# Values of dilation groups 1 and 2: strided token-major products, or feature-major products that are reordered and transposed

## The chip, the cores and the metric

The kernel runs on one core of one Trainium2 chip. The metric is device time in microseconds (us), from the start of the program to its end, as a median of several runs. Engines are named as the profile names them: PE is the matrix engine (PEld its loads of stationary operands, which run beside its products), DVE the vector engine, ACT the scalar engine, POOL GpSimd, and SP the engine that issues most transfers.

## The reference, cut to what matters

The program computes four layers on 512 tokens of 1024 features: a recurrent layer with dilated attention, a layer of sparse attention, and two layers with differential attention and 16 experts. The change touches the first layer alone. There each token gets 12 heads of 128 features in three groups of four; group 0 attends to neighbours, group 1 to every 4th token, group 2 to every 16th:

```
DIL_GROUPS = ((128, 1), (512, 4), (2048, 16))
h = rms_norm(x, norm_g) @ w_in
xa, za, q, k, v, zb, qm, zm = split_cols(h, HAWK_IN_SPLITS)
...
def to_sub(t):          # group gi, dilation dil
    t = t[:, :, gi * DIL_HEADS:(gi + 1) * DIL_HEADS]
    return t.reshape(b, sub, dil, DIL_HEADS, hd).transpose(0, 2, 3, 1, 4).reshape(
        b * dil, DIL_HEADS, sub, hd)
o, lse = banded_attention(to_sub(q)[:, :, None], to_sub(k), to_sub(v), ...)
```

So the values `v` of groups 1 and 2 are wanted with the tokens reordered: all tokens t with the same t mod 4 together.

## The kernel before

All float32 products with weights are made from two float32r parts: an operand is hi + lo, and a product is three matmuls, hi hi, hi lo and lo hi. `x` is kept feature-major, as 8 tiles of 128 features by 512 tokens, in both parts. Weights come by `wcols` in two chunks of 4 row tiles by 256 columns: SP loads a chunk into `wr` (4 buffers), ACT casts it to `wh` (L163, 3 buffers), DVE subtracts for `wl` (L164, 3 buffers).

There are two ways to multiply. `fm` (L184 to L186) takes the weights as the stationary operand and gives 128 columns of the weights on the partitions and 512 tokens along them: 24 matmuls of 512 moving columns fill one PSUM tile `pj`, two tiles a call. `tm2` (L211 to L213) takes 128 tokens of `x` as the stationary operand and 256 weight columns as the moving one: 48 matmuls of 256 columns fill one `pj` with two token tiles, token-major.

`dilated` runs twice (head slots 0 and 1, then 2 and 3; called spans here). A span makes queries and keys of group after group with `fm`, for which ACT (L667, L669) and DVE (L676, L678) copy PSUM to `dq` and `dk`; in groups 1 and 2 that copy also reorders the tokens to (t mod 4, t div 4), reading PSUM with a step of 4 elements. Scores and softmax follow. The weights of the three groups are then mixed through DRAM (`sd`, `wa`, L714 to L733). Then come the values, group 0, 1, 2 (L737 to L745): four token tiles a group, token-major, by `tm2`, which ACT copies to `dv` (L744). For groups 1 and 2 the stationary operand is a view of `x` that takes every fourth token: 128 elements with a step of 4 float32. Last come the transposes of the softmax tiles `de` (L759, copied by ACT to `pT`, L761), the products with the values into `po` (L769), and the gate `zw` by `fm`.

A scheduler sets the order on each engine from the order of the code and the dependences; pools hold 3 `pj` and 2 `pt` tiles of PSUM, and 26 tiles `t2` of 128 by 512 in SBUF.

Of the kernel before, what the change touches and what calls it, by code (L numbers as in the profile page):

```python
# [18 lines left out]
P = 128  # L19
# [29 lines left out]
class K:  # L49
# [11 lines left out]
    @contextmanager  # L61
    def phase(self, name, t2, e=(), r=0, pj=3, ps=2, pt=2, po=1):
        """Pools for one part of the network, with its numbers of tiles and of PSUM banks."""
# [16 lines left out]
    def xt(self):  # L80
        """A (hi, lo) pair of feature tiles."""
        t = self.wp.tile([P, 2, 512], F32R, name="x", tag="xt", bufs=8)
        return t[:, 0], t[:, 1]

    def x2(self):
        """A token tile [128, 1024] as two halves."""
        return [self.t2(F32, "x") for _ in range(2)]
# [29 lines left out]
    @contextmanager  # L117
    def after(self, marks):
        """Puts work on the engines of these instructions behind them."""
        with self.tc.issue_after(marks[0].ins), self.tc.issue_after(marks[1].ins):  # L120
            yield
# [16 lines left out]
    def behind(self):  # L138
        """The queue for a load, which goes behind the work of the last expert for a while."""
# [10 lines left out]
    def chunk(self, pieces, kt=4):  # L150
        """pieces: DRAM APs [kt*128, n], columns side by side (256 in all)."""
# [18 lines left out]
    def wcols(self, W, c0, n=256, k0=0, kt=8):  # L170
        """All row tiles of W[:, c0:c0+n] as [(hi, lo)] per row tile."""
# [9 lines left out]
    def mm3(self, ps, a, b, first, last):  # L181
        """ps += (a_hi + a_lo)^T (b_hi + b_lo), all but lo*lo."""
# [5 lines left out]
    def fm(self, w, x, n=512, cols=2):  # L188
        """Feature-major products: yields PSUM tiles [128 columns of W, n]."""
# [7 lines left out]
    def tm(self, w, x, ps):  # L197
        """Token-major product into ps [128 tokens, columns of w], for the feature tiles x of the tokens."""
# [4 lines left out]
    def tm2(self, w, x, toks, ps):  # L203
        """Token-major products of several token tiles side by side in ps, row tile by row tile."""
# [11 lines left out]
    def rsqrt(self, y, v, n):  # L216
        """y = v ** -0.5 on [128, n]."""
# [14 lines left out]
    def rms(self, xs, q=None, eps=1e-6):  # L232
        """rsqrt(mean(x^2) + eps) of token tiles xs (halves): [128, tiles], and as diagonal matrices; q is scratch."""
# [16 lines left out]
    def turn(self, out, x, diag=None):  # L250
        """out = x^T, or x^T diag."""
# [5 lines left out]
    def features(self, xs, i0, out, g=None, b=None, diag=None):  # L257
        """Two token tiles (halves), the first of them i0, to columns of the feature-major (hi, lo) tiles out, scaled by g
        (and b added); diag scales the tokens."""
# [33 lines left out]
    def constants(self):  # L293
        """The identity and the first norms' gains, then (after a yield) the other vectors."""
# [40 lines left out]
    def distances(self, causal):  # L335
        """Distance (or, if causal, 0) of key from query, and a far-off value where the key may not be seen."""
# [14 lines left out]
    def mem_x(self, name, gain, halves=None, pair=None):  # L351
        """The memory, normalised if gain is given (with the same factors at a second time), as feature-major (hi, lo)
        tiles [128, 256]."""
# [30 lines left out]
    def mem_kv(self, x, W, hd):  # L384
        """Keys of the 4 heads, [128, 256] (hi, lo) (64-wide heads doubled onto both halves), and values per memory tile."""
# [30 lines left out]
    def dup(self, ps, hs, ls):  # L416
        """Two 64-row heads in ps: each head's (hi, lo) doubled onto both partition halves."""
# [7 lines left out]
    def qstack(self, ps, scale, n=512):  # L425
        """Two 64-row heads in ps: per head a tile with its hi part on one half and its lo part on the other."""
# [11 lines left out]
    def scores(self, ps, q, kh, kl, i, n):  # L438
        """ps[:, :n] = scores of query tile i; q is a stack, or (hi, lo)."""
# [10 lines left out]
    def softmax_neg(self, e, ps, bias, m, l, scale=1.0):  # L450
        """e = exp(-scale (ps + bias) - max), l = its row sums; m keeps -max. ps holds negated scores / scale."""
# [5 lines left out]
    def mem_weights(self, q, kv, h):  # L457
        """Transposed weights of head h's attention over the memory."""
# [1497 lines left out]
```

## Time and profile before

| | |
|---|---|
| median of 3 runs | 3067.94 us |
| lowest and highest run | 3065.9 and 3076.09 us |
| span of the profiled execution | 3065.5 us |
| PE busy in it | 2933.4 us, 96% |
| DVE, ACT, POOL busy | 1944.0, 1555.6, 271.6 us |

The profiled execution has its times from the first to the last instruction; the median of the runs lies 2.4 us above that span. The two stretches in which the values of groups 1 and 2 are multiplied are 112.10 to 156.90 us and 283.32 to 328.12 us. PE starts a matmul before the one ahead of it has ended, so the time that one takes in a row of its kind is the distance of two starts, not the duration beside it.

### The profile page before, as it was taken

What the parts mean: (1) busy time and instruction counts of PE and PEld (TensorE: products, weight loads), DVE (VectorE), ACT (ScalarE), POOL (GpSimd) and SP (SyncE); (2) the same over time, 40 slices, a digit from 0 to 9 for tenths busy, and PEclk for the clock granted to TensorE, in tenths of its full rate; (3) what the DMA queues carried; (4) which work ended last, traced back from release to release, by engine and by line L of the source; (5) the groups of instructions that cost most, each with busy time, mean ns of one, the idle gap of its engine ahead of it and who ended that gap; (6) DMA issues with size and microseconds to landing.
All of it is one profiled execution on the core that took longest, in us unless ns stands there. A gap on an engine that the chain in (4) does not pass through costs nothing. (4 is left out here: it accounts for less than half of the span.)

```text
span 3065.5 us, 44383 instructions
## 1 busy us (share of the span) xinstructions
PE 2933.4 (96%) x16795; PEld 2500.5 (82%) x16795; DVE 1944.0 (63%) x3801; ACT 1555.6 (51%) x2717; POOL 271.6 (9%) x282
## 2 busy tenths in 40 slices
PE   8999999999999999999998999969999999699996
PEld 6989887986768999878798888759987878688874
DVE  4353357757756787443467877988744345777788
ACT  4243348546655455322345777735442233467774
POOL 0000000000000000000015200350000000270022
PEclk9999999999999999999999999989999999899998
DMA  4242132541105422222264999942222334369986
GB/s 135 67 143 77 52 114 93 180 135 35 46 21 180 127 63 63 83 93 93 90 204 140 323 327 338 318 142 63 63 76 90 96 110 158 120 242 323 331 323 239
DMA packets 335601, 453.49 MB, mean 148 GB/s; under 512 B 24375, under 2 KB 208409, under 8 KB 335385
## 3 DMA queue, kind: packets, MB, share of 16 engines
q1 hardware_dynamic: 320856, 421.78, 41.5%
q10 hardware_dynamic: 12224, 20.46, 1.8%
q0 software_dynamic: 2304, 8.39, 0.8%
q8 instruction: 133, 2.18, 0.3%
q14 instruction: 84, 0.68, 0.1%
HBM read 421.69 MB, written 28.88 MB: 147 GB/s over the span
## 5 line engine op out<-in xcount | busy, mean ns | idle before, releaser
L164 DVE TENSOR_TENSOR wl<-wr,wh 128x1024 fp32r<-128x1024 f32 x348 | 423.5, 1219 | 502.4 <-ACT wh L163 498.3
L163 ACT CAST wh<-wr 128x1024 fp32r<-128x1024 f32 x352 | 363.1, 1033 | 584.3 <-PE pj L185 316.9
L184 PE MATMUL pj<-x,wh 128*128 128x512 f32 x1224 | 483.4, 395 | 0.6 <-ACT x L110 0.6
L186 PE MATMUL pj<-x,wl 128*128 128x512 f32 x1224 | 481.6, 393 | 0.6 <-DVE wl L164 0.5
L185 PE MATMUL pj<-x,wh 128*128 128x512 f32 x1224 | 482.0, 394 | 0.0
L211 PE MATMUL pj<-wh,x 128*128 128x256 f32 x992 | 299.5, 302 | 3.8 <-DVE xb L277 3.1
L212 PE MATMUL pj<-wl,x 128*128 128x256 f32 x992 | 297.7, 300 | 0.0
L213 PE MATMUL pj<-wh,x 128*128 128x256 f32 x992 | 295.8, 298 | 0.0
L186 PEld LDWEIGHTS pj<-x,wl 128*128 128x128 f32 x1224 | 229.9, 188 | 52.4 <-issue 4.7
L185 PEld LDWEIGHTS pj<-x,wh 128*128 128x128 f32 x1224 | 230.0, 188 | 50.0 <-issue 5.6
L184 PEld LDWEIGHTS pj<-x,wh 128*128 128x128 f32 x1224 | 230.0, 188 | 49.7 <-issue 4.2
L211 PEld LDWEIGHTS pj<-wh,x 128*128 128x128 f32 x992 | 208.1, 210 | 5.2 <-DVE xb L277 3.5
L212 PEld LDWEIGHTS pj<-wl,x 128*128 128x128 f32 x992 | 208.4, 210 | 0.4
L213 PEld LDWEIGHTS pj<-wh,x 128*128 128x128 f32 x992 | 208.2, 210 | 0.3
L211 PE MATMUL pj<-wh,yh 128*128 128x256 f32 x640 | 180.8, 283 | 0.3 <-ACT yh L114 0.2
L212 PE MATMUL pj<-wl,yh 128*128 128x256 f32 x640 | 178.9, 280 | 1.5 <-DVE wl L164 1.5
L213 PE MATMUL pj<-wh,yl 128*128 128x256 f32 x640 | 178.5, 280 | 0.4 <-DVE yl L127 0.3
L1606 DVE TENSOR_TENSOR wl<-mr,wh 128x1024 fp32r<-128x1024 f32 x106 | 139.0, 1312 | 21.0 <-ACT wh L1605 20.9
L1628 PE MATMUL pt<-oh,x 128*128 128x256 f32 x1088 | 136.0, 286 | 15.5 <-DVE oh L1684 8.6
L1606 DVE TENSOR_TENSOR ml<-mr,mh 128x1024 fp32r<-128x1024 f32 x108 | 136.0, 1259 | 21.5 <-ACT mh L1605 18.7
L1628 PEld LDWEIGHTS pt<-oh,x 128*128 128x128 f32 x1088 | 134.8, 194 | 17.5 <-DVE oh L1684 8.7
L1408 POOL TENSOR_TENSOR x<-x,bc 128x512 f32<-128x512 f32 x14 | 18.2, 1320 | 1250.4 <-ACT x L1317 1250.4
(499 smaller groups left out, 6580.4 us busy)
## 6 DMA issues: line engine op xcount, KB each, us to landing
wr<-in_w_in SPq DMA_DIRECT2D x124, 512.0 KB, 3.8
mr<-in_w_exp_gate SPq DMA_DIRECT2D x76, 512.0 KB, 6.9
mr<-in_w_exp_up SPq DMA_DIRECT2D x72, 512.0 KB, 5.3
mr<-in_w_exp_down SPq DMA_DIRECT2D x66, 512.0 KB, 6.1
wr<-in_w_exp_down SPq DMA_DIRECT2D x62, 512.0 KB, 6.1
wr<-in_hawk_w_in SPq DMA_DIRECT2D x60, 512.0 KB, 3.6
wr<-in_w_exp_up SPq DMA_DIRECT2D x56, 512.0 KB, 4.9
wr<-in_w_exp_gate SPq DMA_DIRECT2D x52, 512.0 KB, 6.3
```

Of the source, the lines that this page charges most:

```text
L163: self.nc.scalar.copy(wh[:, :kt, :c], raw[:, :kt, :c])
L164: eng.tensor_tensor(wl[:, :kt, :c], raw[:, :kt, :c], wh[:, :kt, :c].bitcast(F32), op=OP.subtract)
L184: mm(ps, a[0], b[0], start=first, stop=False)
L185: mm(ps, a[0], b[1], start=False, stop=False)
L186: mm(ps, a[1], b[0], start=False, stop=last)
L211: mm(d, tok(x[k][0]), w[k][0][:, :n], start=k == 0 and a == 0, stop=False, skip_group_check=True)
L212: mm(d, tok(x[k][0]), w[k][1][:, :n], start=False, stop=False, skip_group_check=True)
L213: mm(d, tok(x[k][1]), w[k][0][:, :n], start=False, stop=end, skip_group_check=True)
L1408: getattr(nc, eng[0]).tensor_tensor(t[v], x[v], gb[0][v], op=OP.mult)
L1606: self.nc.vector.tensor_tensor(wl, raw, wh.bitcast(F32), op=OP.subtract)
L1628: nc.tensor.matmul(pt[:, u * n:(u + 1) * n], xs[i][part][:, f], oh[:, i], start=i == 0 and part == 0, stop=i == 3 and part == 1)
```

## The change

The values of group 0 stay as they are. Those of groups 1 and 2 are multiplied by `fm`: 128 value features on the partitions, 512 tokens along them, from the unstrided `x`. ACT copies each `pj` to a new tile `vf`, and reorders the tokens in that copy as it does for the queries. PE then transposes the four blocks of 128 tokens into one `pt` tile, and DVE copies these into `dv` in two instructions of 2 by 128 columns. Elsewhere the diff only takes out docstrings and comments; lines behind the change are numbered 11 higher.

```diff
             w = self.wcols(W, 5120 + g * 512 + sp * 256)
-            for i in range(0, 4, 2):
-                ps = self.pj()
-                toks = [(lambda u, b=b: u[:, (i + b) * P:(i + b + 1) * P]) if g == 0 else (
-                    lambda u, b=b: u.rearrange("p (j f) -> p f j", f=4)[:, i + b]) for b in range(2)]
-                self.tm2(w, x, toks, ps)
-                nc.scalar.copy(v[i // 2], ps.rearrange("p (i c) -> p i c", i=2))
+            if g == 0:
+                for i in range(0, 4, 2):
+                    ps = self.pj()
+                    self.tm2(w, x, [lambda u, b=b: u[:, (i + b) * P:(i + b + 1) * P] for b in range(2)], ps)
+                    nc.scalar.copy(v[i // 2], ps.rearrange("p (i c) -> p i c", i=2))
+            else:
+
+                for b, ps in enumerate(self.fm(w, x)):
+                    vf = self.t2(F32, "vf")
+                    nc.scalar.activation(vf.rearrange("p (f j) -> p f j", f=4), ps.rearrange("p (j f) -> p f j", f=4),
+                                         AF.Copy)
+                    pt = self.pt()
+                    for i in range(4):
+                        nc.tensor.transpose(pt[:, i * P:(i + 1) * P], vf[:, i * P:(i + 1) * P], self.ident)
+                    for h in range(2):
+                        nc.vector.tensor_copy(v[h][:, :, b * P:(b + 1) * P],
+                                              pt[:, h * 256:(h + 1) * 256].rearrange("p (i c) -> p i c", i=2))
             vt.append(v)
```

On PE, at the end of the values of a span, before: the last strided products, the transposes of `de`, two products of the gate, and the products into `po`.

```order
L211 MATMUL pj<-wh,x 128x256
L212 MATMUL pj<-wl,x 128x256
L213 MATMUL pj<-wh,x 128x256
L759 MATMUL pt<-ident,de 128x128 x7
L184 MATMUL pj<-x,wh 128x512
L185 MATMUL pj<-x,wh 128x512
L759 MATMUL pt<-ident,de 128x128 x8
L769 MATMUL po<-pT,dv 128x128 x15
L186 MATMUL pj<-x,wl 128x512
```

The same place now; ahead of the first row stand the last product of group 2 and six more of the gate.

```order
L184 MATMUL pj<-x,wh 128x512
L752 MATMUL pt<-ident,vf 128x128 x4
L770 MATMUL pt<-ident,de 128x128 x4
L185 MATMUL pj<-x,wh 128x512
L186 MATMUL pj<-x,wl 128x512
L184 MATMUL pj<-x,wh 128x512
L770 MATMUL pt<-ident,de 128x128 x7
L780 MATMUL po<-pT,dv 128x128
L770 MATMUL pt<-ident,de 128x128 x4
L780 MATMUL po<-pT,dv 128x128 x14
```

The transposes of `vf` never stand right behind the products that they need. In a span the four groups of them come 4, 7, 4 and 7 matmuls behind the end of their product, and the `de` transposes are cut into three pieces.

On ACT, from the second copy of group 0 to the first copy of `pT`, before:

```order
L744 COPY dv<-pj 128x512
L163 CAST wh<-wr 128x1024
L744 COPY dv<-pj 128x512
L163 CAST wh<-wr 128x1024
L744 COPY dv<-pj 128x512
L163 CAST wh<-wr 128x1024
L744 COPY dv<-pj 128x512
L163 CAST wh<-wr 128x1024
L744 COPY dv<-pj 128x512
L761 COPY pT<-pt 128x512
```

And now:

```order
L743 COPY dv<-pj 128x512
L163 CAST wh<-wr 128x1024
L748 ACTIVATE vf<-pj 128x512
L163 CAST wh<-wr 128x1024 x2
L748 ACTIVATE vf<-pj 128x512 x2
L163 CAST wh<-wr 128x1024 x2
L748 ACTIVATE vf<-pj 128x512
L772 COPY pT<-pt 128x512
```

Each group's second `vf` copy stands behind both casts for the weights that come next.

On DVE, from the second chunk of group 1 to the first gate, before and after as one piece of the difference (the rows ahead of it, 20 scalings of `de`, are the same in both):

```order
-L164 TENSOR_TENSOR wl<-wr,wh 128x1024 x4
+L754 COPY dv<-pt 128x2x128 x2
+L164 TENSOR_TENSOR wl<-wr,wh 128x1024 x2
+L754 COPY dv<-pt 128x2x128 x4
+L164 TENSOR_TENSOR wl<-wr,wh 128x1024 x2
+L754 COPY dv<-pt 128x2x128 x2
```

The weights' subtractions now stand behind copies that wait for PE's transposes. Outside these places, in both spans, the order on every engine is that of before.

## Rows read from the trace of the kernel before

**Rows 1.** Busy us (share of the span) and instructions of each engine.

```profile
PE 2933.4 (96%) x16795; PEld 2500.5 (82%) x16795; DVE 1944.0 (63%) x3801; ACT 1555.6 (51%) x2717; POOL 271.6 (9%) x282
```

**Rows 2.** Stretches: length, busy us by engine, granted clock, DMA share, GB/s.

```profile
100.50:112.10 11.60, 11.60 (x99) 11.60 (x98) 4.07 (x28) 6.11 (x22) 0.00 (x0) 1.00 0.29 74
112.10:156.90 44.80, 44.80 (x194) 44.80 (x193) 11.89 (x47) 6.33 (x8) 0.00 (x0) 1.00 0.19 59
283.32:328.12 44.80, 44.80 (x194) 44.80 (x193) 11.22 (x42) 6.33 (x8) 0.00 (x0) 1.00 0.18 59
156.90:175.00 18.10, 18.10 (x125) 16.13 (x125) 4.52 (x5) 7.37 (x13) 0.00 (x0) 1.00 0.11 32
```

**Rows 3.** PE, start and duration in us, from group 0 to group 1.

```profile
111.98 0.28 PE L213 MATMUL pj<-wh,x 128*128 128x256 f32 x1
112.10 0.39 PE L211 MATMUL pj<-wh,x 128*128 128x256 f32 x1
112.33 0.40 PE L212 MATMUL pj<-wl,x 128*128 128x256 f32 x1
```

**Rows 4.** Groups of 112.1 to 156.8 us: busy us, mean ns | idle before.

```profile
L212 PE MATMUL pj<-wl,x 128*128 128x256 f32 x65 | 25.6, 394 | 0.0
L212 PEld LDWEIGHTS pj<-wl,x 128*128 128x128 f32 x64 | 21.1, 329 | 0.0
```

**Rows 5.** Groups of 77.5 to 98.3 us, keys of group 2 among them.

```profile
L185 PEld LDWEIGHTS pj<-x,wh 128*128 128x128 f32 x31 | 5.8, 188 | 1.2
```

**Rows 6.** PE at the end of the keys of group 2, 15 products between.

```profile
94.73 0.39 PE L185 MATMUL pj<-x,wh 128*128 128x512 f32 x1
...
98.36 0.39 PE L186 MATMUL pj<-x,wl 128*128 128x512 f32 x1
```

**Rows 7.** PE behind the values of the first span.

```profile
156.90 0.93 PE L759 MATMUL pt<-ident,de 128*128 128x128 f32 x7
...
158.23 1.09 PE L759 MATMUL pt<-ident,de 128*128 128x128 f32 x8
159.16 3.51 PE L769 MATMUL po<-pT,dv 128*128 128x128 f32 x30
```

**Rows 8.** Groups of 0 to 360 us on ACT and DVE that read PSUM.

```profile
L669 ACT ACTIVATE dq<-pj 128x512 f32<-128x512 f32 x8 | 4.7, 593 | 7.2 <-PE pj L186 7.2
L667 ACT ACTIVATE dq<-pj 128x512 f32<-128x512 f32 x4 | 2.4, 592 | 5.0 <-PE pj L186 5.0
L761 ACT COPY pT<-pt 128x512 f32<-128x512 f32 x12 | 6.7, 599 | 0.0
L125 DVE TENSOR_TENSOR mkl<-pj,mkh 64x256 fp32r<-64x256 f32 x8 | 3.4, 422 | 0.2
```

**Rows 9.** DVE in both spans, start and duration in us, wait in brackets.

```profile
98.78 0.69 DVE L678 COPY dk<-pj 128x512 f32<-128x512 f32 x1 [0.59 <-PE pj L186]
...
114.92 1.22 DVE L164 TENSOR_TENSOR wl<-wr,wh 128x1024 fp32r<-128x1024 f32 x1
116.05 4.27 DVE L754 TENSOR_SCALAR de<-de,ww 128x128 f32<-128x128 f32 x20
...
285.46 1.22 DVE L164 TENSOR_TENSOR wl<-wr,wh 128x1024 fp32r<-128x1024 f32 x1
```

**Rows 10.** ACT, the cast of the second chunk that follows the keys of group 2.

```profile
98.56 1.04 ACT L163 CAST wh<-wr 128x1024 fp32r<-128x1024 f32 x1 [1.62 <-PE pj L185]
```

**Rows 11.** The stretch behind the first span with the most DMA, columns as in Rows 2.

```profile
195.00:217.00 22.00, 21.44 (x106) 17.59 (x106) 15.17 (x50) 9.97 (x15) 0.00 (x0) 1.00 0.79 271
```

**Rows 12.** PE behind a pause elsewhere, start and duration, pause in brackets.

```profile
1338.86 0.97 PE L184 MATMUL pj<-yh,wh 128*128 128x512 f32 x3 [1.99 <-ACT yh L112]
...
1341.27 0.63 PE L184 MATMUL pj<-yh,wh 128*128 128x512 f32 x1
1341.69 0.63 PE L185 MATMUL pj<-yl,wh 128*128 128x512 f32 x1
```

**Rows 13.** One stretch behind that pause, columns as in Rows 2.

```profile
1341.00:1342.00 1.00, 1.00 (x4) 0.81 (x3) 1.00 (x3) 1.00 (x3) 0.00 (x0) 0.50 0.82 289
```

## The prediction

> **What bounds the kernel now.** I read the busy times first: PE works 96% of the span, no other engine more than 63% [rows 1]. So the question is what PE does in the two stretches that the change touches, and whether it waits there. [...] They are the values of groups 1 and 2, 192 matmuls of 256 columns in each span.
>
> Busy is not the same as well used, so I next read the distances of starts. Group 0 runs the same helper at 0.12 us a matmul; at 112.10 us, where group 1 begins, the distance becomes 0.23 us, on the same line, with the same shape [rows 3]. 44.80 us over 192 is 0.2333 us. The one thing that differs is the stationary operand, now every fourth token. The groups show where the time goes: a weight load of the strided operand takes 329 ns [rows 4], one of unstrided weights 188 ns [rows 5], and PEld is busy for the whole of both stretches [rows 2]. So here the loads set the pace, and the 256 columns stream while the next load still runs. Products of 512 columns run at (98.36 - 94.73) / 16 = 0.2269 us [rows 6]: twice the columns in less time than a strided product takes.
>
> **The change part by part, on PE.** Removed: the two stretches, 2 x 44.80 = 89.6 us [rows 2]. Nothing else of PE's lies inside them.
>
> Added: 96 products of 512 columns a span instead of 192 of 256, 192 in all, at 0.2269 us [rows 6]: 43.6 us. They are the very form of the query and key products (weights stationary, x moving), so the price is not a guess.
>
> Added: 32 transposes in 8 groups of four. The eight transposes of `de` at 158.23 us take 0.93 us up to the next operation, 0.116 us each [rows 7]; four are 0.47 us, and I round up to 0.5 us for the change of operation behind them: 4.0 us. The `de` transposes are the same in number but cut into one more piece, and the `po` products too; I put 0.2 us a span on that, 0.4 us.
>
> PE's own sum: 89.6 - 43.6 - 4.0 - 0.4 = 41.6 us less.
>
> **What must keep up.** The first wait is at the start of group 1. Before, the second chunk of its weights was wanted after 24 matmuls of 0.233 us. Now each row tile is used up in three products of 0.2269 us, and the lo part of the fifth is wanted by the 15th product, 112.10 + 14 x 0.2269 = 115.28 us. DVE delivers it at 114.92 + 1.22 = 116.14 us [rows 9], since small operations of the groups' weights stand ahead of it; nothing ahead of that moves. PE stands 0.9 us. In the second span it is wanted at 286.50 and there at 286.68 us [rows 9]: 0.2 us. Together 1.1 us.
>
> Next, the transposes of `vf`. They need the copy by ACT, which begins about 0.42 us after the start of the last product (98.36 to 98.78 us on DVE, the same wait for the same kind of tile) [rows 6, 9] and takes 0.593 us [rows 8]: 1.01 us. The first half's transposes stand 4 products behind, so they are due 5 x 0.2269 = 1.13 us after that start: covered. The second half's copy is queued on ACT behind the cast of the next second chunk, which can only begin when the last product has let go of the old chunk: in the keys 0.20 us after that start, for 1.04 us [rows 6, 10]. Cast and copy end at 0.20 + 1.04 + 0.59 = 1.83 us; the transposes are due 8 x 0.2269 = 1.82 us after it. That is a tie, so I put 0.1 us on each of the four. What hides all this is the 4 or 7 products between; with that cover gone each stop would cost the whole 1.0 to 1.8 us.
>
> DVE's copies to `dv`: two of 2 x 128 columns a tile. No row has this form; a DVE read of 256 PSUM columns with one more operand takes 0.422 us [rows 8], and one of 512 columns 0.69 us [rows 9], so 0.35 to 0.42 us, 16 of them, 6.7 us on an engine that is busy 11.9 of 44.8 us there [rows 2]. Queued behind them are the `wl` subtractions of the next weights. Those wait for a buffer that PE lets go of 12 products (2.7 us) into a tile's second half, by when copies that begin near 1.13 + 0.5 us are done at about 2.4 us. I count nothing; were they late, PE would wait the difference for its next weights. At the end of a span two `de` transposes wait for a free `pt` tile, one on DVE's copy and one on a `pT` copy of 0.599 us [rows 8], with products between; I take 0.5 us a span, 1.0 us, from bounds of 0 and 1.2 us.
>
> The scaling of `de` ends at 116.05 + 4.27 = 120.32 us [rows 9]. Its transposes came at 156.90 us [rows 7]; now they come near 112.1 + 0.9 + 21.8 + 2.0 = 137 us. Still 16 us to spare, so the detour of the groups' weights through DRAM stays hidden.
>
> Waits: 1.1 + 0.4 + 1.0 = 2.5 us. Bounds: nothing at all, or eight uncovered copies of 1.01 us, four uncovered `pT` copies of 0.6 us and the 1.1 us: 11.6 us.
>
> [...] ACT now reads PSUM with a step of four elements. The queries of groups 1 and 2 do just that and take 593 ns; those of group 0 read in order and take 592 ns [rows 8]. [...]
>
> **The sum.** 41.6 - 2.5 = 39.1 us. Everything behind the second span keeps its order, and its loads are issued as buffers come free, not at set times, so I expect it to move as a whole. The sum is made in the profiled execution, span 3065.5 us, which lies 2.4 us under the median of 3067.9 us; with the same distance the forecast is 3029 us, 1.3% less.
>
> **Rivals.**
>
> The stops are not covered. Then 41.6 - 11.6 = 30.0 us remain, 3038 us. For it: four of the eight stops are ties by my sum. Against it: the keys show the same casts and copies in the same order, with PE busy throughout.
>
> The gain of the first span is given back. Behind it come constants, clears of memory and the memory's keys, where DMA is busy at 0.79 and PE stands 0.56 of 22 us [rows 11]. If that stretch were tied to something with a fixed time, 19.6 us would go, 3049 us. Against it: these steps are released by the span's last splits and by buffers, so they come earlier too.
>
> The stride is not the cause. If 0.2333 us belonged to these values and not to the view, the new products would take 192 x 0.4666 = 89.6 us, and transposes and waits would be on top: 3068 + 4.4 + 2.5 = 3075 us. Against it: 329 against 188 ns for one shape of load [rows 4, 5].
>
> [...]
>
> **How the numbers follow.** Forecast 3029 us with 0.81; uncovered stops 0.10; given back 0.04; not the stride 0.03; the clock 0.02. The forecast's bounds are 41.6 us (no waits, 3026) and 30.0 us (all waits, 3038); the three runs lie from 2.0 us under to 8.1 us over their median, so I add 2 us on each side: 3024 to 3040 us, which takes in the first rival and leaves out 0.09, and some more for what I have not thought of. A difference under about 0.3%, 9.2 us, cannot be told from none here. Faster by more: the first three cases, 0.95. Within: not the stride, 0.03. Slower: the clock, 0.02.
>
> **What would show it.** Right: the values of groups 1 and 2 take about 24 to 26 us a span instead of 44.8; distances of 0.227 us between their products; ACT's `vf` copies near 593 ns; PE idle under 2.5 us there, most of it for `wl` in the first span; the rest of the program 39 us earlier, unchanged. Wrong: transposes that wait a microsecond each for ACT; copies near 1.2 us; a granted clock under 1 in the two stretches; a PE pause behind the first span that grew by about 20 us.

## The result and the profile after

The changed kernel takes **3036.57 us** (median of 4 runs, 3030.04 to 3038.98), the kernel before, on the same chip, 3069.56 us (4 runs, 3065.90 to 3076.09). The ratio is 0.9886, with a 95% interval of 0.9874 to 0.9898: 1.1% faster, 33.0 us. A second measurement (a1 below) gave 0.9891 [0.9876, 0.9906]. The forecast was 3029 us with a range of 3024 to 3040. The direction and the range hold; the time lies 7.6 us above the forecast, 6 us of the forecast gain of 39 are missing, and the profiled run of after, at 3038.98 us with a span of 3037.2, is the slowest of its four.

Busy us (share of the span) and instructions of each engine in after, to be held against [rows 1]:

```profile
PE 2896.9 (95%) x16635; PEld 2454.0 (81%) x16635; DVE 1951.3 (64%) x3817; ACT 1557.7 (51%) x2717; POOL 271.0 (9%) x282
```

PE has 160 matmuls fewer (192 x 2 strided products became 192, and 32 transposes came), DVE 16 instructions more. DVE's number turns out to matter, and PE's probably too, for a reason that the prediction did not have.

Stretches of after: length, then busy us (and count) of PE, PEld, DVE, ACT and POOL, granted clock, DMA share, GB/s. They answer to [rows 2]:

```profile
112.38:137.20 24.82, 24.82 (x118) 20.13 (x116) 14.27 (x54) 7.94 (x10) 0.00 (x0) 1.00 0.32 93
137.20:156.00 18.80, 18.80 (x131) 16.87 (x131) 4.72 (x7) 6.19 (x11) 0.00 (x0) 1.00 0.24 75
262.60:287.50 24.90, 24.90 (x119) 20.46 (x119) 13.99 (x54) 7.54 (x10) 0.00 (x0) 1.00 0.30 88
```

The values of groups 1 and 2 now take 24.8 and 24.9 us instead of 44.8, PE is busy for all of it, and the granted clock is 1.00. PEld, which was busy for the whole of both stretches before, has a fifth of them free: the loads no longer set the pace.

PE in after around the first transposes of `vf`, start and duration in us; the spacing answers to [rows 6]:

```profile
118.30 0.39 PE L186 MATMUL pj<-x,wl 128*128 128x512 f32 x1
118.53 0.39 PE L184 MATMUL pj<-x,wh 128*128 128x512 f32 x1
118.76 0.61 PE L752 MATMUL pt<-ident,vf 128*128 128x128 f32 x4
119.12 0.48 PE L185 MATMUL pj<-x,wh 128*128 128x512 f32 x1
```

Products are 0.23 us apart, four transposes take 0.36 us up to the next product, and nothing stands in brackets: PE does not wait for ACT's copy.

Groups of 100 to 345 us in after, the two new kinds of copy: busy us, mean ns | idle before. They answer to [rows 8]:

```profile
L748 ACT ACTIVATE vf<-pj 128x512 f32<-128x512 f32 x8 | 4.8, 595 | 17.1 <-PE pj L186 17.1
L754 DVE COPY dv<-pt 128x256 f32<-128x256 f32 x16 | 6.0, 418 | 9.0 <-PE pt L752 9.0
```

### The profile page after: what moved, and what is told of

It reads as the page before. It is cut to its first block, busy times and chain, and to the rows that moved or that the text cites. A ratio compares the mean times of both kernels' runs of the same rounds, so it can differ in the third digit from the quotient of the medians.

```text
span 3037.2 us, 44080 instructions
## 1 busy us (share of the span) xinstructions
PE 2896.9 (95%) x16635; PEld 2454.0 (81%) x16635; DVE 1951.3 (64%) x3817; ACT 1557.7 (51%) x2717; POOL 271.0 (9%) x282
## 3 DMA queue, kind: packets, MB, share of 16 engines
q1 hardware_dynamic: 320856, 421.78, 42.1%
## 5 line engine op out<-in xcount | busy, mean ns | idle before, releaser
L184 PE MATMUL pj<-x,wh 128*128 128x512 f32 x1288 | 508.2, 395 | 0.6 <-ACT x L110 0.6
L185 PE MATMUL pj<-x,wh 128*128 128x512 f32 x1288 | 507.6, 394 | 0.0
L186 PE MATMUL pj<-x,wl 128*128 128x512 f32 x1288 | 506.3, 393 | 1.1 <-DVE wl L164 1.0
L186 PEld LDWEIGHTS pj<-x,wl 128*128 128x128 f32 x1288 | 241.9, 188 | 54.9 <-issue 4.7
L184 PEld LDWEIGHTS pj<-x,wh 128*128 128x128 f32 x1288 | 242.0, 188 | 52.6 <-issue 4.6
L185 PEld LDWEIGHTS pj<-x,wh 128*128 128x128 f32 x1288 | 242.0, 188 | 52.3 <-issue 5.6
L211 PE MATMUL pj<-wh,x 128*128 128x256 f32 x864 | 249.1, 288 | 3.8 <-DVE xb L277 3.1
L212 PE MATMUL pj<-wl,x 128*128 128x256 f32 x864 | 247.2, 286 | 0.0
L213 PE MATMUL pj<-wh,x 128*128 128x256 f32 x864 | 245.3, 284 | 0.0
L211 PEld LDWEIGHTS pj<-wh,x 128*128 128x128 f32 x864 | 166.3, 193 | 5.2 <-DVE xb L277 3.5
L212 PEld LDWEIGHTS pj<-wl,x 128*128 128x128 f32 x864 | 166.6, 193 | 0.4
L213 PEld LDWEIGHTS pj<-wh,x 128*128 128x128 f32 x864 | 166.3, 193 | 0.3
```

What stands on the lines that cost most here:

```text
L184: mm(ps, a[0], b[0], start=first, stop=False)
L185: mm(ps, a[0], b[1], start=False, stop=False)
L186: mm(ps, a[1], b[0], start=False, stop=last)
L211: mm(d, tok(x[k][0]), w[k][0][:, :n], start=k == 0 and a == 0, stop=False, skip_group_check=True)
L212: mm(d, tok(x[k][0]), w[k][1][:, :n], start=False, stop=False, skip_group_check=True)
L213: mm(d, tok(x[k][1]), w[k][0][:, :n], start=False, stop=end, skip_group_check=True)
```

## Where the gain went on its way to the end

So the stretches do what the prediction says. To see what becomes of the gain, I took the same matmul in two traces and compared its start: how many us earlier it is than in b1, the kernel before run again. "Behind span 2" is the last `po` product of the second span; the other columns are named by their time in b1.

| kernel | behind span 2 | 1632 | 1679 | 2752 | 2811 | 3024 | PE matmuls | DVE instr. |
|---|---|---|---|---|---|---|---|---|
| before (first trace) | 0.4 | -1.3 | -1.2 | -0.9 | -0.9 | -0.3 | 16795 | 3801 |
| after | 41.7 | 37.1 | 32.2 | 31.8 | 27.6 | 28.5 | 16635 | 3817 |
| a1 (after again) | 41.4 | 39.0 | 34.7 | 33.7 | 29.5 | 30.2 | 16635 | 3817 |
| s1 (no stride) | 44.2 | 40.5 | 39.9 | 39.2 | 39.3 | 39.0 | 16795 | 3801 |
| t1 (no transposes) | 46.3 | 44.2 | 43.0 | 42.1 | 38.1 | 39.6 | 16603 | 3817 |
| p1 (copy in order) | 41.9 | 38.7 | 36.3 | 35.4 | 31.9 | 32.8 | 16635 | 3817 |
| c1 (no cover) | 34.7 | 35.0 | 33.0 | 31.8 | 27.9 | 28.8 | 16635 | 3817 |
| m1 (strided moving) | -2.6 | -4.3 | -9.6 | -10.6 | -14.5 | -13.0 | 16635 | 3817 |
| p16 (before + 16 on DVE) | 0.5 | -3.0 | -3.1 | -3.0 | -7.2 | -6.2 | 16795 | 3817 |
| qa (copies on ACT) | 41.7 | 38.1 | 33.6 | 31.7 | 31.7 | 31.7 | 16635 | 3801 |
| pp (after + PE fill) | 31.7 | 28.7 | 26.6 | 28.6 | 25.5 | 26.4 | 16955 | 3817 |
| qp (qa + 160 on PE) | 32.0 | 22.4 | 22.7 | 22.8 | 22.8 | 22.7 | 16795 | 3801 |
| q32 (qa + 32 on PE) | 42.2 | 38.4 | 37.3 | 36.0 | 36.0 | 37.2 | 16667 | 3801 |

The first row is a second trace of b1's kernel: differences of about 1 us are there without any change.

41 to 42 us are gained behind the second span, more than the 39.1 that were forecast. Then it comes off in places: some 2.5 us between 927 and 993 us, then in after and a1 **4.3 to 4.9 us between 1632 and 1679** (the start of the first layer's experts) and **4.2 us between 2752 and 2811** (the second layer's experts).

The loss between 927 and 993 us is not the change's own: every execution but the two of the kernel before has 0.8 to 3.3 us of it, p16 and s1 too. A part of it is PE's clock. All traces have a pause of PE of 1.33 to 1.34 us there, for DVE's `mx`; behind it the granted clock stays 1.00 in before and b1 and falls to 0.50 in every other trace. The same place in before and in after (columns as above):

```profile
934.10:937.10 3.00, 3.00 (x27) 2.85 (x25) 3.00 (x8) 2.67 (x8) 0.00 (x0) 1.00 0.00 0
890.50:893.50 3.00, 3.00 (x16) 3.00 (x15) 2.43 (x6) 1.64 (x4) 0.00 (x0) 0.50 0.00 0
```

Why the clock falls in some traces and not in others, and what the rest of this loss is, stays open.

Experiments on what the other two losses are follow the ones on the stretch itself. Theory C, which the expectations of the later runs name, is this: an engine's instructions come late at such a place, and whether they do depends on how many the engine has had.

## Experiments on the stretch itself

**b1** is the kernel before and **a1** the kernel after, both run once more as measures.

> The kernel before once more, unedited. Theory A (the experts' start varies by itself): against its own first trace its products drift apart by several us behind 1560 us, while they agree within 0.5 us up to there; the ratio is 1.00. Theory B: the two traces agree within 1 us to the end.

Measured: 3071.31 us, ratio 1.0003 [0.9994, 1.0012]. Its trace and that of before stay within 2 us of each other to the end, and lose nothing against each other at the two places.

> The changed kernel once more, unedited, for a second trace and a narrower interval. Its first trace gains 42 to 44 us on PE up to 1560 us and only 28 at the end. Theory A, the start of each layer's experts varies from execution to execution whatever the kernel: the gain behind the second span is again 41 to 44 us, but the loss behind 1560 us comes out at another size, between 0 and 15 us, and the median lies at 3030 to 3040 us. Theory B, the shift itself makes the experts' start later: the same steps lose the same 3 to 5 us each again.

Measured: 3036.58 us (3034.28 to 3038.66), 0.9891 [0.9876, 0.9906]. The losses come again, 4.3 and 4.2 us (4.9 and 4.2 in after). So, as far as two traces of each kernel can tell, they come with the kernel and not from execution to execution, which speaks against theory A.

**s1: the stride alone taken away**, in the kernel before.

```
-                toks = [(lambda u, b=b: u[:, (i + b) * P:(i + b + 1) * P]) if g == 0 else (
-                    lambda u, b=b: u.rearrange("p (j f) -> p f j", f=4)[:, i + b]) for b in range(2)]
+                toks = [lambda u, b=b: u[:, (i + b) * P:(i + b + 1) * P] for b in range(2)]
```

> The kernel before with the stride alone taken away: the values of groups 1 and 2 are multiplied token-major as they were, but from 128 neighbouring tokens, so that the values stand in the wrong token order. If the strided load is the cause, a product takes 0.120 us as in group 0, each stretch of 44.8 us falls to 23.0, and PE is 43.5 us earlier behind the second span; the time falls by 33 to 43 us. If the cause is not the stride, the distances stay at 0.233 us and the time at 3070.

Measured: 3025.59 us, 0.9853 [0.9838, 0.9868]. Groups of s1 from 112 to 140 us, the lines that took 394 and 329 ns in [rows 4]:

```profile
L212 PE MATMUL pj<-wl,x 128*128 128x256 f32 x64 | 18.1, 283 | 0.0
L212 PEld LDWEIGHTS pj<-wl,x 128*128 128x128 f32 x64 | 12.3, 192 | 0.0
```

With nothing else changed the load falls from 329 to 192 ns, and PE is 44.2 us earlier behind the second span. The stride is the cause; the detour by feature-major products and transposes gets back 41.4 of these 44.2 us.

**t1: the transposes alone taken away**, in after.

```
-                    pt = self.pt()
-                    for i in range(4):
-                        nc.tensor.transpose(pt[:, i * P:(i + 1) * P], vf[:, i * P:(i + 1) * P], self.ident)
...
-                                              pt[:, h * 256:(h + 1) * 256].rearrange("p (i c) -> p i c", i=2))
+                                              vf[:, h * 256:(h + 1) * 256].rearrange("p (i c) -> p i c", i=2))
```

> The changed kernel without the 32 transposes: DVE copies the reordered tile straight into the values, which are then wrong. By my sum the transposes cost PE 4.0 us and their waits 0.4; so the values of a span end 2.0 to 2.2 us earlier than in the changed kernel and the time falls by 4 us, within the scatter. If transposes stop PE for their copies, it falls by 8 us or more.

Measured: 3029.71 us, 0.9867 [0.9852, 0.9882], 6.9 us less than a1. Of this 46.3 - 41.4 = 4.9 us are on the spot, against 4.4 that the prediction gave to transposes and breaks. The other 2 us arise downstream.

**c1: the cover taken away**, in after: the next products stay behind the transposes at three of four places of each span.

```
...
+                    ps = self.pj()
+                    with self.tc.issue_after(mark) if mark else nullcontext():
+                        for k in range(len(w)):
+                            self.mm3(ps, [u[:, b * P:(b + 1) * P] for u in w[k]], x[k], k == 0, k == len(w) - 1)
...
-                        nc.tensor.transpose(pt[:, i * P:(i + 1) * P], vf[:, i * P:(i + 1) * P], self.ident)
+                        mark = nc.tensor.transpose(pt[:, i * P:(i + 1) * P], vf[:, i * P:(i + 1) * P], self.ident).ins
```

> The kernel after, with the next products held behind the transposes at three of the four places of each span, so that no product covers the copy of vf (in after four products of 0.227 us stand ahead of each four transposes). The output is the reference's. If that cover is what makes the copy free: PE pauses about 4 x 0.227 = 0.9 us at each of six places, 5.4 us in all, the gain behind the second span is 36 us in place of 41.4, and the time 3042. By the price the prediction gave to an uncovered stop, 1.0 to 1.8 us, it is 6 to 11 us, 3043 to 3048. Rival (the copy is hidden anyway): 3036.6.

Measured: 3039.31 us, 0.9904 [0.9888, 0.9919]. PE in c1, start and duration, the pause and what ended it in brackets:

```profile
117.60 0.39 PE L186 MATMUL pj<-x,wl 128*128 128x512 f32 x1
118.67 0.66 PE L756 MATMUL pt<-ident,vf 128*128 128x128 f32 x4 [0.69 <-ACT vf L752]
```

The pauses are 0.69 us behind a first half and 1.41 us behind a second half, where ACT's cast stands ahead of the copy; 2 x (0.69 + 1.41 + 0.69) = 5.6 us in a trace, and 41.4 - 34.7 = 6.7 us behind the second span, 1.1 us a stop. So the cover is real, and an uncovered stop costs somewhat less than the 1.0 to 1.8 us that the prediction gave it. At the end the medians are only 2.7 us apart, since c1 loses less than a1 at 927 to 993 (0.8 us against 2.5) and at 1632 to 1679 (1.9 against 4.3): a local loss of a few us cannot be read from the end of this program.

**p1: the copy out of PSUM in order**, in after.

```
-                    nc.scalar.activation(vf.rearrange("p (f j) -> p f j", f=4), ps.rearrange("p (j f) -> p f j", f=4),
-                                         AF.Copy)
+                    nc.scalar.activation(vf, ps, AF.Copy)
```

> The kernel after, with the values of groups 1 and 2 copied out of PSUM in order, not reordered (so the values stand in the wrong token order, and the output differs). It prices ACT's read of PSUM with a step of four: if a row of after is right (vf 595 ns reordered, and the rows of before for copies in order, 592), nothing changes: 41.4 us gained behind the second span, 3036.6. Rival (the step costs something that the mean hides, on ACT or by holding the bank against PE): the copies are shorter, and the gain up to 1 us larger; 3035.

Measured: 3036.64 us, 0.9890 [0.9875, 0.9905]; 41.9 us behind the second span. Groups of 100 to 345 us in p1:

```profile
L748 ACT ACTIVATE vf<-pj 128x512 f32<-128x512 f32 x8 | 4.8, 596 | 17.1 <-PE pj L186 17.1
```

596 ns in order, 595 with the step of four in after: reordering on the way out of PSUM costs ACT nothing here.

**m1: the moving operand strided in place of the copy**, in after.

```
-                for b, ps in enumerate(self.fm(w, x)):
+                xr = [[u.rearrange("p (j f) -> p f j", f=4) for u in t] for t in x]
+                for b in range(2):
+                    ps = self.pj()
+                    for k in range(len(w)):
+                        self.mm3(ps.rearrange("p (f j) -> p f j", f=4), [u[:, b * P:(b + 1) * P] for u in w[k]], xr[k],
+                                 k == 0, k == len(w) - 1)
...
+                    nc.scalar.activation(vf, ps, AF.Copy)
```

> The kernel after, but the values of groups 1 and 2 are reordered by the products: their moving operand is read with a step of four tokens, and ACT copies the PSUM tile in order. Transposes and copies stay, and the output is the reference's. If only a stationary operand is slowed by the step: 192 products of 512 columns at 0.2269 us as in after, 41 us gained behind the second span, 3036 us. If a step of four slows whatever is read with it, by what the stationary ones show (0.141 us for 128 columns), a product takes 0.2269 + 4 x 0.141 = 0.79 us, 192 of them 108 us more, and the time is 3145 us. ACT's copy of a tile is 0.59 us in both.

Measured: 3081.76 us, 1.0035 [1.0024, 1.0045], slower than before. PE in m1, and the stretch that these rows come from (columns as above):

```profile
113.43 0.65 PE L184 MATMUL pj<-x,wh 128*128 128x512 f32 x1
113.89 0.64 PE L185 MATMUL pj<-x,wh 128*128 128x512 f32 x1
114.35 0.65 PE L186 MATMUL pj<-x,wl 128*128 128x512 f32 x1
```

```profile
113.43:121.00 7.57, 7.57 (x18) 3.52 (x17) 5.58 (x22) 0.00 (x0) 0.00 (x0) 1.00 0.32 102
```

Both expectations missed. The products are 0.46 us apart at a granted clock of 1.00, against 0.23 us: the step costs this moving operand time too, a factor of two, and (41.4 + 2.6) / 192 = 0.229 us a product by the table. It is less than the estimate from the stationary loads, 0.79 us. Whichever operand of the product was read with the step, PE paid: 329 ns a load in place of 192 (s1), 0.46 us a product in place of 0.23. The engines that copied out of PSUM did not: ACT took 595 ns with the step and 596 in order (p1), DVE 691 and 689 ns for the tiles of `dk` in before.

## Experiments on the two losses downstream

What DVE does in after at the second loss; qa, below it, is there at the same time within 0.11 us. DVE, start and duration, its idle time in brackets:

```profile
2728.49 1.22 DVE L1617 TENSOR_TENSOR ml<-wr,mh 128x1024 fp32r<-128x1024 f32 x1
2729.89 1.22 DVE L1617 TENSOR_TENSOR wl<-mr,wh 128x1024 fp32r<-128x1024 f32 x1 [0.17 <-ACT wh L1616]
2735.81 1.23 DVE L1617 TENSOR_TENSOR ml<-wr,mh 128x1024 fp32r<-128x1024 f32 x1 [4.70 <-ACT wh L1616]
```

And in qa:

```profile
2728.59 1.22 DVE L1617 TENSOR_TENSOR ml<-wr,mh 128x1024 fp32r<-128x1024 f32 x1
2729.99 1.22 DVE L1617 TENSOR_TENSOR wl<-mr,wh 128x1024 fp32r<-128x1024 f32 x1 [0.17 <-ACT wh L1616]
2731.85 1.23 DVE L1617 TENSOR_TENSOR ml<-wr,mh 128x1024 fp32r<-128x1024 f32 x1 [0.64 <-ACT mh L1616]
```

ACT's cast that this subtraction needs runs at the same time in both:

```profile
2730.68 1.04 ACT L1616 CAST mh<-wr 128x1024 fp32r<-128x1024 f32 x1
```

```profile
2730.78 1.04 ACT L1616 CAST mh<-wr 128x1024 fp32r<-128x1024 f32 x1
```

In qa DVE goes on 0.03 us after the cast's end; in after it stands 4.1 us longer with its operands ready, so the releaser in its bracket is not what it waited for. PE in after runs dry behind it, and the stretch after the pause is at half the clock (columns as above):

```profile
2734.17 0.39 PE L184 MATMUL pj<-mh,xgh 128*128 128x512 f32 x1
2737.09 0.79 PE L185 MATMUL pj<-ml,xgh 128*128 128x512 f32 x1 [2.54 <-DVE ml L1617]
2737.68 0.63 PE L186 MATMUL pj<-mh,xgl 128*128 128x512 f32 x1
2738.11 0.63 PE L184 MATMUL pj<-mh,xgh 128*128 128x512 f32 x1
```

```profile
2732.00:2734.00 2.00, 2.00 (x11) 1.60 (x10) 0.00 (x0) 1.70 (x2) 0.00 (x0) 1.00 1.05 399
2737.10:2740.00 2.90, 2.90 (x7) 2.32 (x8) 2.90 (x3) 0.37 (x1) 0.00 (x0) 0.50 0.54 177
```

A pause of 2.54 us, then products 0.43 us apart at a granted clock of 0.50, until about 2740: 2.5 us of pause and 8 products that cost 0.2 us more make the 4.2 us. The DMA share is 1.05 from 2732 to 2734 us, while DVE stands.

**p16: 16 DVE instructions more, and nothing else**, in before.

```
                 nc.scalar.copy(v[i // 2], ps.rearrange("p (i c) -> p i c", i=2))
+                if g > 0:
+                    for _ in range(2):
+                        nc.vector.memset(self.small([16], name="rs"), 0.0)
```

> The kernel before, with 16 fills of a small tile (128x16) by DVE put in where the values of groups 1 and 2 are copied out (four for each group of each span). Nothing reads them, and the output is the reference's. DVE then has 3817 instructions, as after has, and nothing else is changed. Theory C (DVE stands at one place of the second layer's experts because its next instructions come late, and where that falls depends on how many it has had): PE is as in before up to 2700 us, then a stop of about 4 us of DVE, and of PE behind it, appears in the experts of the second layer, as in after, a1 and t1; 3075 us, against 3071 of before. Rival (the stop comes from the weights' transfers being earlier by 30 to 40 us): no stop, 3071.

Measured: 3073.79 us, 1.0012 [1.0002, 1.0021]. DVE in p16:

```profile
2770.41 1.23 DVE L1609 TENSOR_TENSOR ml<-wr,mh 128x1024 fp32r<-128x1024 f32 x1 [4.53 <-ACT wh L1608]
```

The same subtraction stands 4.53 us, and PE loses 4.2 us between 2752 and 2811, though PE is no earlier than in before (0.5 us behind the second span) and the 16 fills are done some 2400 us ahead.

**qa: the 16 copies on ACT instead of DVE**, in after.

```
-                        nc.vector.tensor_copy(v[h][:, :, b * P:(b + 1) * P],
-                                              pt[:, h * 256:(h + 1) * 256].rearrange("p (i c) -> p i c", i=2))
+                        nc.scalar.copy(v[h][:, :, b * P:(b + 1) * P],
+                                       pt[:, h * 256:(h + 1) * 256].rearrange("p (i c) -> p i c", i=2))
```

> The kernel after, with the 16 copies of the transposed values from PSUM done by ACT, not by DVE; DVE then has 3801 instructions, as before has, ACT 16 more. Locally about as after, since the copies lie beside products on either engine: 41 us gained behind the second span. Theory C: DVE's stop of 4.2 us in the second layer's experts goes, the loss of 4.3 us at the first layer's experts stays; 3032 us, if ACT with its 16 more gets no such stop of its own. Rival (stops come from transfers being earlier): 3036.6, as a1.

Measured: 3034.42 us, 0.9881 [0.9864, 0.9897], 2.2 us under a1, which the overlapping intervals do not tell apart; the traces do. The stop is gone (31.7 us before and behind it). Over all the kernels: the eight with 3817 DVE instructions lose 3.1 to 4.2 us between 2752 and 2811, and before, b1, s1, qa, qp and q32 with 3801 lose nothing (under 0.1 us), whatever else was changed and however early they were.

Now the first loss. There PE starts on the first expert. Start and duration in after, of DVE's work on `oh`, the matrix that picks the expert's tokens, and of the PE work on it:

```profile
1613.44 1.72 DVE L1650 TENSOR_SCALAR oh<-iota,rank 128x128 fp32r<-128x128 f32 x8 [4.08 <-ACTq L1688]
```

```profile
1617.62 16.72 PE L1639 MATMUL pt<-oh,x 128*128 128x256 f32 x128 [5.28 <-ACT mh L1616]
```

PE begins 4.18 us behind DVE's start. In before, b1, s1, t1, p1, p16, pp, qp and q32 it is 1.15 to 1.17 us; in a1, qa, m1 and c1 3.58, 3.74, 3.76 and 2.14 us.

This late begin, up to 3.0 us, is one part of the loss; the other goes with the clock again. In the 6 us from PE's begin the granted clock is 1.00 in before, b1, s1, t1, p16 and qp, and 0.52 to 0.74 in the other eight, also in p1 and pp, where PE begins on time. Those 6 us in b1, p1 and after (columns as above):

```profile
1650.80:1656.80 6.00, 5.92 (x48) 5.71 (x48) 4.70 (x8) 5.99 (x7) 6.00 (x7) 1.00 0.24 74
1613.52:1619.52 6.00, 6.00 (x38) 6.00 (x39) 4.70 (x8) 5.99 (x8) 6.00 (x7) 0.73 0.25 75
1617.62:1623.62 6.00, 6.00 (x39) 6.00 (x40) 4.24 (x5) 3.72 (x5) 6.00 (x7) 0.74 0.79 262
```

In b1 and p1 PE's pause ahead of them is the same, 2.25 and 2.27 us. With the late begin taken off, the loss is 0.9 to 2.7 us in the eight with the lower clock and at most 1.1 us in the six others.

**pp: PE's number of matmuls raised**, in after.

```
                     pt = self.pt()
+                    for _ in range(20):
+                        nc.tensor.matmul(pt[:1, :1], self.ident[:, :1], self.ident[:, :1], start=True, stop=True)
```

> The kernel after, with 160 products of one column put ahead of the transposes (20 ahead of each four), so that PE has as many matmuls as before has (16795). Nothing reads them, and the output is the reference's. They cost something on the spot, up to some 0.1 us each, which the gain behind the second span tells (41.4 us in a1). Theory C for PE (how late PE is at the first of the first layer's experts depends on how many instructions it has had): of the 4.3 to 4.9 us that after and a1 lose between 1632 and 1679 us not more than 1 is left, and DVE's 4.2 us in the second layer stay. Rival: both losses stay as in a1.

Measured: 3042.88 us, 0.9911 [0.9895, 0.9928]. My count was wrong: a float32 product of one column appears twice, so PE has 16955 matmuls, not 16795. They cost 41.4 - 31.7 = 9.7 us on the spot, 0.03 us each. The first loss is 2.1 us, not the 1 us at most that was expected, and not the 4.3 of a1; DVE's is 3.1 us. PE begins on time, and the 2.1 us come behind that, at the lower clock. With a number that is not before's, it decides nothing by itself.

**qp: PE and DVE both at before's numbers**, in qa.

```
             nc.tensor.transpose(ps[:, :n], src[:n], self.ident[:n, :n])
+            if r is rows[0]:
+                pad = self.pt()
+                for _ in range(160):
+                    nc.tensor.transpose(pad[:, :2], self.ident[:2], self.ident[:2, :2])
```

> The kernel qa (after with ACT copying the transposed values), with 160 transposes of two columns put where PE waits for its first data, behind the first transpose of the program (4.10 us; PE's next work starts at 10.23 in qa). Nothing reads them, and the output is the reference's. PE and DVE then have as many instructions as in before (16795 and 3801). Theory C: both losses go: nothing at the second layer's experts as in qa, and at the first of the first layer's experts at most 0.7 us in place of 4.6, as in before, s1 and p16, which have the same count; 3034.4 - 4 = 3030 us, and the fastest with the reference's output so far. If the 160 take over 0.038 us each, the first block of transposes starts late by what is over. Rival (the loss at the first layer comes from transfers that are earlier, and the count is chance): 3034.4 as qa.

Measured: 3043.48 us, 0.9915 [0.9901, 0.9928]. PE at the start of qp:

```profile
3.99 17.20 PE L330 MATMUL pt<-ident 2*128 2x2 f32 x160
21.12 3.78 PE L255 MATMUL pt<-diag,x 128*128 128x128 f32 x16
```

As a faster version it fails: the fill took 0.108 us a piece, 17.2 us in all, where 6 were free, and waits moved elsewhere, which I put down to its extra PSUM tile (6.6 us go between 587 and 634, with a pause of 3.43 us of PE for DVE's `x` and the clock at 0.50 behind it). As a test it fits: from 1632 us to the end nothing is lost (22.4 to 22.7 us), for the first time with the changed values; PE begins on time and the clock stays 1.00. But it gets there 16 us later than qa, which could be the reason too.

**q32: as qp, with 32 matmuls that cost 0.03 us each, in the same PSUM tile**, in qa.

```
             nc.tensor.transpose(ps[:, :n], src[:n], self.ident[:n, :n])
+            if r is rows[0]:
+                pad = ps[:, 511:512]
+                for _ in range(16):
+                    nc.tensor.matmul(pad[:1, :1], self.ident[:, :1], self.ident[:, :1], start=True, stop=True)
```

> The kernel qa with 16 products of one column (two passes of PE each, so 32 matmuls in the trace, some 0.03 us each by pp) behind the first transpose of the program, where PE waits for data from 4.1 to 10.2 us anyway. Nothing reads them, and the output is the reference's. PE then has 16667 matmuls, 128 fewer than before, s1, p16 and qp, which lose up to 0.7 us at the first of the first layer's experts; after, a1, qa and m1 with 16635 lose 4.3 to 5.4, t1 with 16603 1.1, pp with 16955 2.1. In b1 the queue that brings PE's code has 133 packets for 2 x 16795 matmuls and weight loads, one for some 126 matmuls. Theory C (what counts is where PE stands between two such packets): 128 fewer is the same place, the loss at 1679 us is at most 0.7, nothing else is lost that qa doesn't lose, and the time is 3034.4 - 4.2 = 3030 us. Rival 1 (the loss follows the count evenly): about 0.8 of it stays, 3033.5. Rival 2 (qp lost nothing there because it was 15 us later, not because of its count): 3034.4 as qa.

Measured: **3028.47 us** (3026.67 to 3031.60), 0.9866 [0.9849, 0.9882]. The start of q32, and the place of the first loss, in PE and DVE:

```profile
4.17 0.94 PE L330 MATMUL pt<-ident 128*1 128x1 f32 x32
10.91 3.78 PE L255 MATMUL pt<-diag,x 128*128 128x128 f32 x16 [5.81 <-DVE diag L246]
```

```profile
1612.40 16.87 PE L1643 MATMUL pt<-oh,x 128*128 128x256 f32 x128 [2.26 <-DVE oh L1654]
```

```profile
1611.24 1.72 DVE L1654 TENSOR_SCALAR oh<-iota,rank 128x128 fp32r<-128x128 f32 x8 [4.08 <-ACTq L1692]
```

The fill lies in PE's wait for the first data, PE begins on the first expert 1.16 us behind DVE, and 1.1 us are lost between 1632 and 1679 (0.7 were expected at most, 4.6 in qa), at a granted clock of 0.72 in the 6 us from PE's begin. It comes there as early as qa (38.4 and 38.1 us), so being later is not what helped qp. Next to s1, whose values stand in the wrong order, it is the fastest kernel here: 41 us under before, 8 us under after, though the ends of the two intervals against before still touch (0.9849 to 0.9882 and 0.9874 to 0.9898).

**What is shown and what is not.** That DVE's stop hangs on the number of DVE's instructions ahead of it, and on nothing else tried, is shown by p16 and qa. That PE's late begin hangs on PE's number is likely: five of six executions with 16635 matmuls begin 2.1 to 4.2 us behind DVE, in place of 1.15 to 1.17, and none of the eight with another number; but p1, with 16635, is on time. The rest of the first loss, all of it in p1 and pp, goes with the lower clock, which pp and q32 have with other numbers; why the clock falls there in some traces only stays open.

That the engines wait there for their code is an inference of mine that no run shows, though the times fit closely. The page of after has two queues of the kind "instruction" (packets, MB, share of 16 engines):

```profile
q8 instruction: 132, 2.16, 0.3%
q14 instruction: 83, 0.68, 0.1%
```

132 packets of q8, 16 KB each, beside 2 x 16635 matmuls and loads of PE are one for 252 of them, and their number goes with PE's: 132 at 16603 to 16667 matmuls, 133 at 16795, 134 at 16955. In all eight traces with DVE's stop, DVE goes on 1.53 to 1.57 us behind the end of a packet of q14 (2734.27 and 2735.81 us in after, 2768.88 and 2770.41 in p16); the six traces without the stop have no packet of q14 within 10 us of that subtraction. In the five traces where PE begins late, it begins 2.66 to 2.76 us behind the end of a packet of q8 (1614.86 and 1617.62 us in after). In p1 that distance is 2.67 us too, but there the packet ended 1.5 us ahead of DVE's start, so it held up nothing. Which engine a queue serves, the profile does not say; that one of them brings PE's code, as the expectation of q32 has it, rests on the kind and on these numbers alone. No run changed the packets alone: the cause of the two stops is not shown.

## Why the prediction was right, and where not

**What bounds the kernel**: right. The strided load set the pace: without the stride it took 192 ns in place of 329, and PE was 44.2 us earlier (s1).

**PE's sum**, 41.6 us: right. 89.6 us became 49.7 for both stretches (24.82 + 24.90; 12 of a span's 16 transposes and some of the gate's products lie in them), and PE is 41.4 (a1) and 41.7 us (after) earlier behind the second span. Products at 0.227 us, `vf` copies at 595 ns (593 forecast), `dv` copies at 418 ns (350 to 420) came as read from [rows 6, 8]. Transposes and breaks were put at 4.4 us; t1 gives 4.9.

**The waits**, 2.5 us: the term that was mis-sized; it measured nothing. PE does not pause once in either span of after, from its first product of group 1 to its last one into `po`. The largest part was a misreading: I took the subtraction at 114.92 us [rows 9] for the second chunk of group 1. In after it runs from 114.89 to 116.11 us, and PE's 15th product, the first to use that chunk's lo part, starts ahead of its end:

```profile
115.58 0.39 PE L186 MATMUL pj<-x,wl 128*128 128x512 f32 x1
```

```profile
114.89 1.22 DVE L164 TENSOR_TENSOR wl<-wr,wh 128x1024 fp32r<-128x1024 f32 x1
```

So that subtraction is a later chunk's; the one for group 1 stood a place earlier in the queue (111.19 us), there being three buffers, not two. The ties at the second halves went the good way; c1 shows what they would have cost.

**"I expect it to move as a whole"**: the step that failed. In a1 11.2 of 41.4 us are given back behind the second span (41.4 to 30.2), 4.3 and 4.2 of them at two places where an engine stands with its operands ready, and 2.5 between 927 and 993 us. The argument, that loads are issued as buffers come free, was about transfers. It left out two things. The change alters the number of instructions: DVE's (+16) brings the stop of 4.2 us some 2400 us later, and PE's (-160) probably the late begin, 2.4 us in a1 and 3.0 in after, some 1300 us later. And behind pauses that the kernel before has too, PE's clock fell in after where it did not in before (0.50 against 1.00 behind the pause for `mx`, 0.74 against 1.00 in the 6 us from PE's begin on the first expert); the prediction looked for a granted clock under 1 only in the two stretches. q32, with DVE's number back at 3801 and PE's 128 short of before's, at no cost on the spot, runs at 3028.5 us, where the forecast was.

**The two errors lie on opposite sides**: 2.3 us too much for waits, 11.2 us too little for what comes behind. The spans of a1 and b1 are 30.2 us apart, the medians 33 to 35. That the time lies in the range is in part luck: the range's upper end was made of uncovered stops, of which none came, and it had room for losses that the prediction had not thought of.

**The rivals.** Stops uncovered: they are not; c1 prices them at 6.7 us for six, 8.9 for eight, against 8.1 in the bound of 11.6 us (with the prediction's own 1.8 us for a second half, the eight would have been 11.4). The first span's gain given back: no, 20.3 us (a1) are still there at 191 us. Not the stride: s1 excludes it. The clock, the slower case with 0.02: 1.00 in both stretches with 12 transposes in each, and in the 18.8 us behind the first, with 34 more; a lower clock did cost something, but behind pauses further on, of the kind of [rows 12, 13], at 927 to 993 us (0.50) and in the experts (0.74 and 0.50 in after).

## What to carry to other kernels

Here an operand that PE read with a step of four cost PE time, as weights (329 ns a load against 192, s1) and as moving data (0.46 us a product against 0.227, m1), and a detour was worth it (41.4 of 44.2 us on the spot): let ACT reorder the product as it leaves PSUM, and transpose behind a few other products. Price such a detour from the same forms in the profile, and keep products between a PSUM tile's end and the transposes that need its copy, which was worth 1.1 us a place in c1. When a long program gains less at its end than on the spot, line up the same instruction in both traces: a stop with all operands ready, that comes or goes with a handful of dummy instructions far ahead, was none of the change's own waits here, and 4.2 us of the gain hung on it (p16, qa). Compare the granted clock behind the same pause as well: at the first expert the traces with the lower clock lost 0.9 to 2.7 us, the others at most 1.1.

## What the runs showed that I had not expected

- With a step of four float32 tokens a weight load of 128 x 128 took 329 ns, not 192 (s1), and a product with a moving operand of 512 columns 0.46 us, not 0.227 (m1).
- ACT's copy of a PSUM tile with that step: 595 ns, in order 596 (p1).
- 16 idle DVE instructions cost 4.2 us of PE, some 2400 us later (p16); ratio 1.0012 [1.0002, 1.0021].
- Behind a pause of PE of 2.25 to 2.27 us the granted clock was 1.00 in b1 and 0.73 in p1, as means of the next 6 us.
- DVE's stop ended 1.53 to 1.57 us behind a packet of kind "instruction", in all eight traces that have it.
- PE instructions whose result nothing read took time: 0.03 us for each pass of one column (pp, q32), 0.108 us for a transpose of 2 x 2 with weights of 128 columns (qp).
